# Loading the gate weights in a thread of their own, and letting the first output tile begin before the last head's weights are ready

## The chip, the cores and the metric

The kernel runs on one core of a Trainium2 chip. The metric is the device time of one execution in microseconds (us). Three runs of the kernel before gave 402.6, 404.37 and 405.15; their median is 404.37. The engines are TensorE (PE, with PEld for its weight loads), VectorE (DVE), ScalarE (ACT), GpSimd (POOL) and SyncE (SP), which issues the DMAs here.

## The reference, cut to what matters

One layer that runs differential attention (four heads) and a bidirectional S5 state-space model (SSM) side by side over 512 sample tokens and 128 prompt tokens of 1024 channels. The change touches only the end of the layer:

```python
m = silu(cond) @ w_ada + b_ada                  # shift, scale, gate = thirds of m, one set for
                                                # the sample tokens and one for the prompt tokens
w = softmax(q1 k1) - lam * softmax(q2 k2)       # per head
o = rmsnorm(w @ v, subln) * (1 - lam_init) * silu(g_attn)            # 512 channels, four heads
ys = ys * sigmoid(ys @ w_glu + b_glu) * silu(g_ssm)                  # 512 channels, the SSM gate
out = concat([o, ys]) @ w_out                   # 640 x 1024 times 1024 x 1024
y = x + gate * rmsnorm(out, norm_post)
```

The gate's weights (`w_gate` in the kernel) are the last third of `w_ada`, 1024 x 1024 in fp32, that is eight blocks of 512 KB. `w_out` and `x` are read in blocks of 512 KB too, eight of `w_out` and five of `x`.

## The kernel before, in words

**Threads and the planner.** The program is a list of some fifty generators ("threads"), each with a priority number (line 1572 ff.; lower goes first). When the kernel is built, a planner (`Machine.run`) asks every thread for its next instruction, works out with a table of its own costs when that could start, and takes the earliest; among those that are within a small tie it takes the lowest priority number. What comes out is one fixed order of instructions for each engine. On the chip every engine keeps to its order and only waits for data. A thread waits in the planner for events (`yield from on(...)`), which another thread sets with `did(...)`.

**Memory.** SBUF is cut into named regions; `sb(..., at="T1 T2")` takes room in the first of these regions where the planner finds it free, `drop` gives it back. The eight PSUM banks are handed out by `bank(...)` and given back by `undo`. The profile shows tiles by region (`sb_T`, `sb_S`, `sb_RAW`, ...), and every engine instruction has line 270 there, since a single helper records them all; tiles tell them apart.

**Around the change.** Late in the program these threads run side by side:
- `scores`, `values`, `finish`: for each of four heads, score blocks of 128 rows, a softmax on ACT and DVE, transposes of the weights, products with the values (128x128 matmuls `sb_T,sb_WH`), then the norm of the head's result on DVE and ACT, four transposes back (`sb_S,sb_WH`), the gating, and a split into two parts. Event `("w", h, b)` says that block b of head h has its weights; blocks have another order than their numbers, and `("w", 3, 4)` belongs to the last head.
- `glu`: the gate of the SSM branch; its event is "glu".
- `gates` (line 1427): four rounds. A round loads two `w_gate` blocks (512 KB each) into regions T1 and T2, multiplies each with the conditioning vectors (`ada_mm`, eight matmuls of 32 columns per block, which the trace shows as sixteen rows), adds the bias on DVE, splits the sum on ACT and DVE, spreads it over 128 rows with four selector matmuls of 256 columns (`sb_RX`), and multiplies it on DVE by `norm_post` into `gp`. In each round bias and norm are loaded by two small DMAs of their own, from the same SP queue as everything else.
- `wo_load`, `wo_split`: the eight `w_out` blocks are loaded into RAW, RX or T2 and split into two tiles each. `x_load`: the five blocks of `x` for the residual.
- `output` (line 1497): five output tiles of 128 tokens. The first four have 48 matmuls of 128x512 each: eight input blocks k in `ORDER = (4, 5, 0, 1, 6, 7, 2, 3)`, two halves of the columns, and three products of split numbers (high x high, high x low, low x high). Blocks 4 to 7 of `z` come from the SSM gate, blocks 0 to 3 from the heads, so block 3, the last in the order, waits for the last head. Each tile takes a pair of PSUM banks. `out_after` norms a tile, multiplies by `gp`, adds `x` and stores it.

The last head's result passes: the last value matmul, a copy on DVE, a sum of squares on ACT, twelve small DVE instructions for its norm, three scalings, four transposes, the gating, the split, and then the six matmuls of block 3 in the first output tile.

Of the kernel before, what the change touches and what calls it, by code (L numbers as in the profile page):

```python
# [11 lines left out]
OP = mybir.AluOpType  # L12
# [334 lines left out]
def layer(m, pst, dr, I, O, V, A, P, S, T):  # L347
    sizes = {}

    def sb(*shape, dt=F32, at="S", low=True, step=1):  # L350
        n = -(-math.prod(shape) // 8) * 8
        ap, at = yield lambda: m.take(n, dt, at.split(), low, step)
        sizes[at] = n
        ap = ap[:, 0:math.prod(shape)]
        if dt == I32:
            ap = ap.bitcast(dt)
        if len(shape) > 1:
            nm = "abcd"[:len(shape)]
            ap = ap.rearrange("p (%s) -> p %s" % (" ".join(nm), " ".join(nm)), **dict(zip(nm[1:], shape[1:])))
        return ap  # L360

    def sbs(n, *shape, **k):
        o = []
        for _ in range(n):
            o.append((yield from sb(*shape, **k)))
        return o

    def drop(*aps):
        for ap in aps:
            at = m.box(ap)[0]  # L370
            m.give(at, sizes.pop(at))
# [105 lines left out]
    g = {}  # L477
# [949 lines left out]
    def gates():  # L1427
        yield from on(("w_q", 3, 1), ("v", 1, 2))
        gp = g["gpost"] = yield from sb(2, 1024, at="T1", low=False)
        sel = yield from sb(2, 128)  # L1430
        bt, npo = yield from sbs(2, 256, at="T1", low=False)
        yield S.dma_start(sel, I["sel"])
        yield V.memset(bt, 0.0)
        sr, hi, lo = yield from sbs(3, 256, dt=F32R, at="RX")
        yield A.activation(sr, flat(sel), AF.Copy)
        drop(sel)
        for i in range(4):
            r = slice(256 * i, 256 * i + 256)
            yield S.dma_start(bt[0:2], bass.AP(tensor=I["b_gate"].tensor, offset=I["b_gate"].offset + 256 * i,
                                               ap=[[0, 2], [1, 256]]))  # L1440
            yield S.dma_start(npo, bass.AP(tensor=I["npost"].tensor, offset=I["npost"].offset + 256 * i,
                                           ap=[[0, 128], [1, 256]]))
            ps = yield from bank((4, 5, 6, 7))
            for j in range(2):
                wa = yield from sb(8, 128, at="T1 T2")
                yield S.dma_start(wa, I["w_gate"][2 * i + j])
                yield from ada_mm(ps[:, 128 * j:128 * j + 128], wa, 128)
                drop(wa)
            rg = yield from sb(256)
            yield V.tensor_tensor(rg, ps[:, 0:256], bt, op=OP.add)  # L1450
            undo(ps)
            yield from split(hi, lo, rg)
            drop(rg)
            ps = yield from bank((4, 5, 6, 7))
            for v in range(2):
                o = ps[:, 256 * v:256 * v + 256]
                for n, x in enumerate((hi, lo)):
                    yield T.matmul(o, sr[:, 128 * v:128 * v + 128], x, start=(n == 0), stop=(n == 1))
            yield V.tensor_tensor(gp[:, :, r], ps.rearrange("p (a b) -> p a b", a=2),
                                  npo[:, None].to_broadcast([128, 2, 256]), op=OP.mult)  # L1460
            undo(ps)
        drop(bt, npo, sr, hi, lo)
        did("gates")


    ORDER = (4, 5, 0, 1, 6, 7, 2, 3)
# [28 lines left out]
    later3 = []  # L1495

    def output():
        yield from on("glu", ("w", 3, 4))
        for t in range(5):
            q = slice(128 * t, 128 * t + 128)  # L1500
            if t == 3:
                yield from on("gates")
            pr = yield from bank((0, 2, 4, 6), pair=True)
            ps = [pr[:, 0], pr[:, 1]]
            if t < 4:
                order = [(n, c) for n in range(8) for c in PIECE[t]]
            else:
                order = [(n, c) for c in PIECE[t] for n in range(8)]
                ps.append((yield from bank((0, 1, 2, 3, 4, 5, 6, 7))))
            ps = [p[:, 0:c.stop - c.start] for p, c in zip(ps, PIECE[t])]  # L1510
            for n, c in order:
                k = ORDER[n]
                yield from on(("z", k), ("wo", k))
                yield from three(ps[PIECE[t].index(c)], [x[:, q] for x in g["z", k]], [x[:, c] for x in g["wo", k]], n == 0,
                                 n == 7)
                if n == 7:
                    did(("out", t, c.start))
                    if c == PIECE[t][1 if t < 4 else 0]:
                        later3.append(out_after(t, ps))
# [45 lines left out]
    def trailing3():  # L1565
        for _ in range(5):
# [5 lines left out]
            (4.0, g_make()), (-2.0, g_turn()), (2.0, follow("g_turn", 16)), (5.0, g_apply()), (4.0, follow("g_apply", 16)), (-8.0, scan()), (0.0, fin()),  # L1572
            (1.0, e_make()), (3.0, e_taps()), (2.0, tz_make()), (0.0, y_in()), (1.0, y_out()), (-2.0, follow("y_out", 8)), (11.0, w_load()), (4.0, w_split()), (13.0, proj()),
            (0.0, trailing()), (TURN, turn()), (5.0, lam_()), (1.0, keys()), (-2.0, scores()), (8.0, values()), (5.0, finish()), (14.0, glu()),
            (2.0, trailing2()), (8.0, gates()), (11.0, wo_load()), (20.0, wo_split()), (24.0, x_load()), (13.0, output()), (9.0, trailing3())]

# [91 lines left out]
```

## Time and profile before

| | |
|---|---|
| runs (median) | 402.6, 404.37, 405.15 us (404.37) |
| the profiled execution | 403.84 us, its span 401.7 us |
| granted TensorE clock, mean over the span | 0.987 |
| PE busy | 377.9 us, 94% of the span |
| DVE busy | 338.1 us, 84% |
| ACT busy | 212.4 us, 53% |
| POOL busy | 19.7 us, 5% |
| DMA | 50.80 MB in the span |

A time in the rows counts from the start of the span, which is shorter than the time of the execution: what lies before its first and behind its last instruction is not in it. Rows of the timelines join neighbouring instructions of one kind (x3 is three of them): the first number is the start of the first, the second the length of the whole piece. Consecutive matmuls overlap, so the step from one piece's start to the next one's tells more than its length.

### The profile page before, as it was taken

To read this page: it belongs to the slowest core of one execution; us is meant where nothing else is said; L and a number is where in the kernel's file an instruction comes from. 1 tells how busy PE (TensorE), PEld (TensorE's weight loads), DVE (VectorE), ACT (ScalarE), POOL (GpSimd) and SP (SyncE) were. 2 spreads that over 40 slices of the span, in tenths; PEclk is the share of its full clock that TensorE was granted. 3 is DMA by queue.
4 is the path that set the end of the run, shared out by engine and by line. 5 is a ranking of instruction groups with operands and counts; after the bars stand their busy time and mean duration, and the time that the engine had idled before them with its cause. 6 is when DMAs were issued, how large, how long until landed. Compare 5 with 4: busy or idle time off the path is not lost.

```text
span 401.7 us, 8863 instructions
## 1 busy us (share of the span) xinstructions
PE 377.9 (94%) x3422; PEld 336.0 (84%) x3422; DVE 338.1 (84%) x964; ACT 212.4 (53%) x473; POOL 19.7 (5%) x30
## 2 busy tenths in 40 slices
PE   6899999999999999999999999999999877999991
PEld 6887899987988889999989899898977755788891
DVE  4999899998999998999999997899988986633453
ACT  4766556599823252323584565798874872311021
POOL 1101000000000000000000220032000020000001
PEclk9899999999999999999999999999999998999998
DMA  7999127540354232131186411054023535132111
GB/s 277 404 407 364 48 60 216 180 130 3 104 164 105 80 131 85 60 104 54 56 194 170 119 35 27 11 187 131 25 87 115 157 130 214 52 106 104 52 54 52
DMA packets 30969, 50.80 MB, mean 126 GB/s; under 512 B 11592, under 2 KB 19792, under 8 KB 29904
## 3 DMA queue, kind: packets, MB, share of 16 engines
q1 hardware_dynamic: 30928, 50.24, 38.6%
q8 instruction: 27, 0.44, 0.5%
q14 instruction: 14, 0.11, 0.1%
HBM read 43.45 MB, written 6.78 MB: 125 GB/s over the span
## 4 chain that ended last, share of the span: by engine, by line
PE 58%; DVE 23%; DMA 10%; ACT 4%; issue 3%; SPq 1%; DVEq 0%; ACTq 0%
PE ps__65 L270 58%; DVE sb_S L270 13%; DMA sb_T<-in_w_gate 7%; ACT sb_WH L270 4%; DVE sb_W L270 3%; DVE sb_WH L270 3%; DMA sb_H<-in_x 1%; DMA sb_RAW<-in_w_gs 1%; DMA sb_S<-dk 1%; DVE sb_Z L270 1%; DVE sb_BC L270 1%; SPq L270 1%; DVE sb_T L270 0%; ACT sb_S L270 0%; DVE sb_RX L270 0%
## 5 line engine op out<-in xcount | busy, mean ns | idle before, releaser
L270 PE MATMUL ps__65<-sb_H,sb_W 128*128 128x320 f32 x864 | 141.9, 316 | 0.0
L270 PEld LDWEIGHTS ps__65<-sb_H,sb_W 128*128 128x128 f32 x864 | 127.7, 188 | 2.7 <-issue 1.4
L270 ACT ACTIVATE sb_WH<-ps__65 128x128 f32<-128x128 f32 (+4 forms) x89 | 39.9, 483 | 32.4 <-PE ps__65 L270 30.7
L270 PE MATMUL ps__65<-sb_H,sb_Z 128*128 128x256 f32 (+2 forms) x247 | 49.1, 332 | 0.0
L270 ACT ACTIVATE sb_W<-sb_RAW 128x1024 fp32r<-128x1024 f32 (+1 forms) x26 | 26.2, 1011 | 40.6 <-PE ps__65 L270 30.5
L270 PEld LDWEIGHTS ps__65<-sb_H,sb_Z 128*128 128x128 f32 x247 | 38.7, 190 | 4.8 <-issue 2.0
L270 DVE TENSOR_REDUCE sb_S<-ps__65 128x1 f32<-128x640 f32 (+2 forms) x48 | 29.5, 622 | 5.0 <-PE ps__65 L270 3.2
L270 ACT ACTIVATE sb_WH<-ps__65,sb_S 128x640 f32<-128x640 f32 (+2 forms) x46 | 31.0, 683 | 4.2 <-DVE sb_S L270 4.0
L270 PE MATMUL ps__65<-sb_S 64*128 64x320 f32 (+2 forms) x258 | 30.5, 320 | 1.0 <-POOL sb_S L270 1.0
L270 PE MATMUL ps__65<-sb_W,sb_S 128*32 128x256 f32 (+2 forms) x184 | 27.6, 378 | 3.8 <-DVE sb_S L270 3.8
L270 DVE TENSOR_TENSOR sb_W<-sb_RAW,sb_W 128x1024 fp32r<-128x1024 f32 (+1 forms) x25 | 28.9, 1155 | 0.1
L270 PE MATMUL ps__65<-sb_S,sb_WH 128*128 128x128 f32 x136 | 26.3, 289 | 2.6 <-DVE sb_S L270 1.3
L270 PEld LDWEIGHTS ps__65<-sb_S 64*128 64x128 f32 (+1 forms) x258 | 25.3, 200 | 3.9 <-issue 1.8
L270 PE MATMUL ps__65<-sb_W,sb_H 128*128 128x512 f32 x120 | 28.3, 392 | 0.0
L270 PEld LDWEIGHTS ps__65<-sb_W,sb_H 128*128 128x128 f32 x120 | 22.3, 188 | 4.7 <-issue 0.2
L270 DVE TENSOR_TENSOR sb_S<-sb_S 128x512 f32<-128x512 f32 (+7 forms) x67 | 20.0, 303 | 7.1 <-DMA sb_S<-in_spar 4.5
L270 PEld LDWEIGHTS ps__65<-sb_W,sb_S 128*32 128x32 f32 (+1 forms) x184 | 18.5, 148 | 8.6 <-DVE sb_S L270 3.9
L270 DVE TENSOR_TENSOR sb_WH<-ps__65,sb_T 128x512 f32<-128x512 f32 (+1 forms) x10 | 6.6, 665 | 21.3 <-ACT sb_RAW L270 15.4
L270 PEld LDWEIGHTS ps__65<-sb_S,sb_WH 128*128 128x128 f32 x136 | 17.1, 152 | 8.4 <-ACT sb_WH L270 3.5
L270 ACT ACTIVATE sb_T<-ps__65 128x512 f32<-128x512 f32 (+2 forms) x31 | 14.9, 490 | 17.4 <-PE ps__65 L270 16.9
L270 DVE SCALAR_TENSOR_TENSOR sb_S<-sb_S 128x1 f32<-128x1 f32 (+5 forms) x117 | 20.3, 186 | 2.4 <-ACT sb_S L270 1.1
L270 DVE SCALAR_TENSOR_TENSOR sb_WH<-sb_WH,sb_S 128x640 f32<-128x640 f32 (+3 forms) x29 | 22.0, 771 | 0.4
(146 smaller groups left out, 624.5 us busy)
## 6 DMA issues: line engine op xcount, KB each, us to landing
sb_W<-in_w_ada SPq DMA_DIRECT2D x6, 1024.0 KB, 11.7
sb_T<-in_w_gate SPq DMA_DIRECT2D x8, 512.0 KB, 4.7
sb_RAW<-in_w_out SPq DMA_DIRECT2D x7, 512.0 KB, 3.8
sb_H<-in_x SPq DMA_DIRECT2D x5, 512.0 KB, 5.1
sb_WH<-in_x SPq DMA_DIRECT2D x5, 512.0 KB, 5.7
sb_T<-in_w_ada SPq DMA_DIRECT2D x2, 1024.0 KB, 13.6
sb_RAW<-in_w_k SPq DMA_DIRECT2D x4, 512.0 KB, 3.3
sb_RAW<-in_w_q SPq DMA_DIRECT2D x4, 512.0 KB, 3.4
```

The source lines that it names most:

```text
L270: r = getattr(self.eng[op.eng], op.name)(*op.args, **op.kw)
```

## The change

Three things are changed in two threads, and one thread is added.
- Bias and norm are loaded once: the norm as a whole row of 1024 straight into the tile `gp`, before the loops, and the bias as one tile of four rows of 256 columns, cleared by a memset that goes from DVE to POOL. The multiply with the norm becomes two instructions per round, of 256 columns each, since its result now overwrites the norm.
- The `w_gate` loads move to a thread `gates_load` with the same priority (8.0), which starts when the room for bias and norm is taken and has no other condition but room in T1 or T2.
- `output` waits for "glu" alone; the wait for `("w", 3, 4)` moves from the first to the second tile. The first tile may now take only banks 4 and 5.

```diff
--- before.py
+++ after.py
@@ -1427,27 +1427,26 @@
     def gates():
         yield from on(("w_q", 3, 1), ("v", 1, 2))
         gp = g["gpost"] = yield from sb(2, 1024, at="T1", low=False)
-        sel = yield from sb(2, 128)
-        bt, npo = yield from sbs(2, 256, at="T1", low=False)
+        yield S.dma_start(gp[:, 0], bass.AP(tensor=I["npost"].tensor, offset=I["npost"].offset, ap=[[0, 128], [1, 1024]]))
+        sel, bt = (yield from sb(2, 128)), (yield from sb(4, 256))
         yield S.dma_start(sel, I["sel"])
-        yield V.memset(bt, 0.0)
+        yield P.memset(bt, 0.0)
+        yield S.dma_start(bt[0:2], bass.AP(tensor=I["b_gate"].tensor, offset=I["b_gate"].offset,
+                                           ap=[[0, 2], [256, 4], [1, 256]]))
+        did("gates room")
         sr, hi, lo = yield from sbs(3, 256, dt=F32R, at="RX")
         yield A.activation(sr, flat(sel), AF.Copy)
         drop(sel)
         for i in range(4):
             r = slice(256 * i, 256 * i + 256)
-            yield S.dma_start(bt[0:2], bass.AP(tensor=I["b_gate"].tensor, offset=I["b_gate"].offset + 256 * i,
-                                               ap=[[0, 2], [1, 256]]))
-            yield S.dma_start(npo, bass.AP(tensor=I["npost"].tensor, offset=I["npost"].offset + 256 * i,
-                                           ap=[[0, 128], [1, 256]]))
             ps = yield from bank((4, 5, 6, 7))
             for j in range(2):
-                wa = yield from sb(8, 128, at="T1 T2")
-                yield S.dma_start(wa, I["w_gate"][2 * i + j])
+                yield from on(("wg", 2 * i + j))
+                wa = g["wgate", 2 * i + j]
                 yield from ada_mm(ps[:, 128 * j:128 * j + 128], wa, 128)
                 drop(wa)
             rg = yield from sb(256)
-            yield V.tensor_tensor(rg, ps[:, 0:256], bt, op=OP.add)
+            yield V.tensor_tensor(rg, ps[:, 0:256], bt[:, i], op=OP.add)
             undo(ps)
             yield from split(hi, lo, rg)
             drop(rg)
@@ -1456,11 +1455,18 @@
                 o = ps[:, 256 * v:256 * v + 256]
                 for n, x in enumerate((hi, lo)):
                     yield T.matmul(o, sr[:, 128 * v:128 * v + 128], x, start=(n == 0), stop=(n == 1))
-            yield V.tensor_tensor(gp[:, :, r], ps.rearrange("p (a b) -> p a b", a=2),
-                                  npo[:, None].to_broadcast([128, 2, 256]), op=OP.mult)
+            for v in (1, 0):
+                yield V.tensor_tensor(gp[:, v, r], ps[:, 256 * v:256 * v + 256], gp[:, 0, r], op=OP.mult)
             undo(ps)
-        drop(bt, npo, sr, hi, lo)
+        drop(bt, sr, hi, lo)
         did("gates")
+
+    def gates_load():
+        yield from on("gates room")
+        for n in range(8):
+            wa = g["wgate", n] = yield from sb(8, 128, at="T1 T2")
+            yield S.dma_start(wa, I["w_gate"][n])
+            did(("wg", n))
 
 
     ORDER = (4, 5, 0, 1, 6, 7, 2, 3)
@@ -1495,12 +1501,14 @@
     later3 = []
 
     def output():
-        yield from on("glu", ("w", 3, 4))
+        yield from on("glu")
         for t in range(5):
             q = slice(128 * t, 128 * t + 128)
             if t == 3:
                 yield from on("gates")
-            pr = yield from bank((0, 2, 4, 6), pair=True)
+            if t == 1:
+                yield from on(("w", 3, 4))
+            pr = yield from bank((0, 2, 4, 6) if t else (4,), pair=True)
             ps = [pr[:, 0], pr[:, 1]]
             if t < 4:
                 order = [(n, c) for n in range(8) for c in PIECE[t]]
@@ -1572,7 +1580,7 @@
             (4.0, g_make()), (-2.0, g_turn()), (2.0, follow("g_turn", 16)), (5.0, g_apply()), (4.0, follow("g_apply", 16)), (-8.0, scan()), (0.0, fin()),
             (1.0, e_make()), (3.0, e_taps()), (2.0, tz_make()), (0.0, y_in()), (1.0, y_out()), (-2.0, follow("y_out", 8)), (11.0, w_load()), (4.0, w_split()), (13.0, proj()),
             (0.0, trailing()), (TURN, turn()), (5.0, lam_()), (1.0, keys()), (-2.0, scores()), (8.0, values()), (5.0, finish()), (14.0, glu()),
-            (2.0, trailing2()), (8.0, gates()), (11.0, wo_load()), (20.0, wo_split()), (24.0, x_load()), (13.0, output()), (9.0, trailing3())]
+            (2.0, trailing2()), (8.0, gates()), (8.0, gates_load()), (11.0, wo_load()), (20.0, wo_split()), (24.0, x_load()), (13.0, output()), (9.0, trailing3())]
 
 
 
```

What this does to the order of instructions is seen at three places. The first is SP's queue from the load of the last cached keys (`in_kc`) on, before and now (`sb_T` and `sb_RAW` are where the blocks go):

```order
L270 DMA sb_S_78<-in_kc 128x128
L270 DMA sb_T_0_188<-in_w_gate 128x1024
L270 DMA sb_T_0_91<-in_w_gate 128x1024
L270 DMA sb_T_0_91<-in_b_gate 2x256
L270 DMA sb_T_0_91<-in_npost 128x256
L270 DMA sb_T_0_91<-in_w_gate 128x1024
L270 DMA sb_T_0_188<-in_w_gate 128x1024
```

```order
L270 DMA sb_S_78<-in_kc 128x128
L270 DMA sb_S_78<-in_sel 128x256
L270 DMA sb_RAW_105<-in_w_out 128x1024
L270 DMA sb_S_78<-in_b_gate 2x1024
L270 DMA sb_T_0_91<-in_w_gate 128x1024
L270 DMA sb_T_0_188<-in_w_gate 128x1024
L270 DMA sb_RAW_105<-in_w_out 128x1024
L270 DMA sb_T_0_91<-in_w_gate 128x1024
L270 DMA sb_T_0_188<-in_w_gate 128x1024
L270 DMA sb_T_0_91<-in_w_gate 128x1024
L270 DMA sb_T_0_188<-in_w_gate 128x1024 x3
L270 DMA sb_WH_79<-in_x 128x1024 x3
```

The first two `w_gate` loads now stand behind the seventh `w_out` load and the bias load; the last four stand together, with three loads of `x` right behind, and no bias or norm load is left among them.

The second place is PE from the last value matmul on (the first row of each piece). Moving tiles `sb_H_1_518`, `sb_W_1_707`, `sb_W_1_753` and `sb_H_1_253` with 512 columns are `w_out` blocks of the first output tile, rows of 32 columns are gate matmuls, `sb_RX` rows the selector matmuls, and `sb_S_78,sb_WH_79` transposes. Before, and now:

```order
L270 MATMUL ps__65<-sb_T_0_188,sb_WH_79 128x128
L270 MATMUL ps__65<-sb_H_1_518,sb_S_1_2565 128x512 x6
L270 MATMUL ps__65<-sb_H_1_518,sb_Z_3157 128x512
L270 MATMUL ps__65<-sb_W_1_707,sb_Z_3157 128x512
L270 MATMUL ps__65<-sb_H_1_518,sb_Z_3157 128x512
L270 MATMUL ps__65<-sb_T_0_91,sb_S_78 32x128 x3
L270 MATMUL ps__65<-sb_S_78,sb_WH_79 128x128
L270 MATMUL ps__65<-sb_T_0_91,sb_S_78 32x128 x5
L270 MATMUL ps__65<-sb_H_1_518,sb_Z_3157 128x512
```

```order
L270 MATMUL ps__65<-sb_T_0_188,sb_WH_79 128x128
L270 MATMUL ps__65<-sb_W_1_753,sb_S_1_2821 128x512
L270 MATMUL ps__65<-sb_H_1_253,sb_S_1_2821 128x512
L270 MATMUL ps__65<-sb_W_1_753,sb_S_1_2821 128x512
L270 MATMUL ps__65<-sb_RX_3679 128x256
L270 MATMUL ps__65<-sb_H_1_253,sb_S_1_2821 128x512
L270 MATMUL ps__65<-sb_RX_3679 128x256 x3
L270 MATMUL ps__65<-sb_H_1_253,sb_S_1_2821 128x512 x3
L270 MATMUL ps__65<-sb_T_0_91,sb_S_78 32x128 x8
L270 MATMUL ps__65<-sb_H_1_253,sb_S_1_2821 128x512 x2
L270 MATMUL ps__65<-sb_T_0_188,sb_S_78 32x128 x8
L270 MATMUL ps__65<-sb_S_78,sb_WH_79 128x128 x4
```

Before, 42 of the first tile's 48 matmuls stood behind the last value matmul. Now 9 stand between it and the last head's four transposes, with the gate matmuls of the fifth and sixth `w_gate` block among them, and 6 behind.

The third place is PE at the start of the first output tile, now (before, that tile's first matmuls stood between the last transposes of attention weights, a few rows ahead of the last value matmul). `sb_S_1_2821 128x320` are the matmuls of score blocks:

```order
L270 MATMUL ps__65<-sb_S_1_2821 128x320 x12
L270 MATMUL ps__65<-sb_T_0_188,sb_WH_79 128x128
L270 MATMUL ps__65<-sb_S_78,sb_WH_79 128x128
L270 MATMUL ps__65<-sb_H_1_518,sb_Z_3157 128x512 x6
L270 MATMUL ps__65<-sb_H_1_518,sb_S_1_2565 128x512 x5
L270 MATMUL ps__65<-sb_S_78,sb_WH_79 128x128 x4
L270 MATMUL ps__65<-sb_H_1_518,sb_S_1_2565 128x512
L270 MATMUL ps__65<-sb_S_1_2821 128x320 x12
```

The tile's first twelve matmuls stand ahead of one of the last head's score blocks, and more of them between the softmax work behind it: 33 of 48 come before the last value matmul.

## Rows read from the trace of the kernel before

**Rows 1.** The page's head and its busy times by engine.
```profile
span 401.7 us, 8863 instructions
PE 377.9 (94%) x3422; PEld 336.0 (84%) x3422; DVE 338.1 (84%) x964; ACT 212.4 (53%) x473; POOL 19.7 (5%) x30
```

**Rows 2.** The chain of waits in order of time: start, length, what.
```profile
329.37 7.21 DMA sb_T<-in_w_gate
336.62 9.22 PE ps__65 L270 x59
...
348.14 45.09 PE ps__65 L270 x220
```

**Rows 3.** PE's timeline: start, length, operation, out<-in, shapes, count, [idle before <-releaser].
```profile
329.52 0.94 PE L270 MATMUL ps__65<-sb_H,sb_Z 128*128 128x512 f32 x3
...
331.55 0.38 PE L270 MATMUL ps__65<-sb_T,sb_WH 128*128 128x128 f32 x2
...
343.14 0.64 PE L270 MATMUL ps__65<-sb_T,sb_S 128*32 128x128 f32 x16
...
345.23 0.60 PE L270 MATMUL ps__65<-sb_S,sb_WH 128*128 128x128 f32 x4
...
349.19 1.55 PE L270 MATMUL ps__65<-sb_H,sb_Z 128*128 128x512 f32 x6
...
358.74 1.52 PE L270 MATMUL ps__65<-sb_H,sb_UY 128*128 128x512 f32 x6
360.10 1.52 PE L270 MATMUL ps__65<-sb_H,sb_Z 128*128 128x512 f32 x6
```

**Rows 4.** PE's waits from 285 us on: us in total, times, longest.
```profile
PE ps__65 L270 <- DMA sb_T<-in_w_gate: 5.7, 5, 2.6
PE ps__65 L270 <- DVE sb_S L270: 1.3, 1, 1.3
PE ps__65 L270 <- ACT sb_WH L270: 0.5, 1, 0.5
PE ps__65 L270 <- DVE sb_WH L270: 0.4, 1, 0.4
```

**Rows 5.** Stretches: length, PE busy (count), granted clock, DMA share, GB/s.
```profile
320.00:334.00 14.00, 11.09 (x90) 1.00 0.49 160
336.70:340.00 3.30, 3.30 (x20) 0.50 0.40 158
```

**Rows 6.** The w_gate loads as one tile: from issue to landing.
```profile
DMA to landing us min/median/max: 3.4/4.7/7.2
```

**Rows 7.** SP's timeline, the issues of loads.
```profile
289.35 0.33 SPq L270 DMA_DIRECT2D sb_T<-in_w_gate  x1
...
317.05 0.33 SPq L270 DMA_DIRECT2D sb_RAW<-in_w_out  x1
```

**Rows 8.** POOL's groups: busy us and mean ns | idle before.
```profile
L270 POOL MEMSET sb_S<- 128x400 f32 (+1 forms) x3 | 0.9, 357 | 0.3 <-POOLq L1656 0.3
```

**Rows 9.** DVE's timeline around the last head's end.
```profile
333.07 0.28 DVE L270 COPY sb_WH<-ps__65 128x128 f32<-128x128 f32 x1
...
344.39 0.17 DVE L270 SCALAR_TENSOR_TENSOR sb_S<-sb_S 128x5 f32<-128x5 f32 x1
344.59 0.68 DVE L270 TENSOR_SCALAR sb_WH<-sb_WH,sb_S 128x128 f32<-128x128 f32 x3
...
345.87 0.75 DVE L270 SCALAR_TENSOR_TENSOR sb_S<-ps__65,sb_S,sb_S 128x512 f32<-128x512 f32 x1 [0.26 <-PE ps__65 L270]
...
347.39 0.69 DVE L270 TENSOR_TENSOR sb_UY<-sb_S,sb_UY 128x512 fp32r<-128x512 f32 x1
```

**Rows 10.** ACT's timeline around the last head's end.
```profile
333.39 0.31 ACT L270 ACTIVATE sb_S<-sb_WH 128x128 f32<-128x128 f32 x1 [0.60 <-DVE sb_WH L270]
333.61 0.19 ACT L270 ACTIVATION_READ_ACCUMULATOR sb_S<-sb_WH 128x1 f32 x1
...
346.65 0.63 ACT L270 ACTIVATE sb_UY<-sb_S 128x512 fp32r<-128x512 f32 x1 [1.28 <-DVE sb_S L270]
```

## The prediction, made before the changed kernel was run

> **What bounds the kernel now.** I read the engines' busy times first, then the chain of waits at its end, then PE's waits, and last the timelines of PE, SP, DVE and ACT around the last head. PE is busy 94% of a span of 401.7 us [rows 1]; the profiled execution took 403.84 us, so 2.14 lie around the span. A kernel like this gets faster only where PE idles, runs slowly, or has its last work made ready late.
>
> The chain ends with one unbroken PE stretch of 45.09 us from 348.14 on, and it goes through w_gate loads before that [rows 2]. The stretch is the second output tile (from 349.19 [rows 3]) and the three after it. The change touches neither these four tiles, but for some matmuls of the gates, nor the 8.5 us behind them. So **its worth is how far it moves the start of the second tile**, now 349.19.
>
> What happens ahead of it? From 285 us on PE waits 5.7 us for w_gate loads in five waits, the longest 2.6, and 1.3 + 0.5 + 0.4 = 2.2 us for DVE and ACT [rows 4]. [...]
>
> **The change, part by part.** *Loads of bias and norm.* Four norm loads and four bias loads become one each. In the old order a norm load stood in the queue just ahead of three of the w_gate pairs; the last of these w_gate loads, issued at 329.37, took 7.21 us to land [rows 2], where the quickest took 3.4 and the median was 4.7 [rows 6]. Six issues of about 0.33 us [rows 7] leave SP, which is no bound. The gain of this edit sits in the waits above.
>
> *The loading thread.* It does not bring the first loads forward. They were issued from 289.35 on; now the queue has the seventh w_out load, and then the bias load, ahead of them. The w_out load waits for DVE to free its buffer, which was at 317.05 [rows 7]. In the new order of DVE that release stands one of the last head's row maxima earlier, so I take 313 to 314 us; the first w_gate issues some 0.8 later and lands at 314.4 + 3.4 to 4.7 = 317.8 to 319.1. PE comes to the first group of gate matmuls just ahead of the last-but-one score block, about 318 to 319. So this wait is nothing to 1 us; I take zero, the upper end stays in the range. Loads 5 to 8 leave when PE frees their buffers, about ten matmuls before they are used.
>
> *The memset on POOL.* Three memsets of up to 400 columns took POOL 0.36 us on average [rows 8]; for 1024 that is at most about 1 us. It is off DVE, and SP waits for w_out at that time anyway. If that cover goes, up to 1 us comes onto the loads. The four multiplies by the norm, one of 512 columns each, become eight of 256: nothing but a start each, beside PE.
>
> *The first tile earlier.* Its 48 matmuls of 128x512 used to start at 329.52 and surround the last value matmul at 331.55 [rows 3]: 6 before it, 42 after. In the new order 33 stand before it and 15 after, 9 of them ahead of the last head's transposes and 6 behind them. Now two things can set the second tile's start, PE's work up to the last value, and the last head's chain after it; I go through both.
>
> Last value: 27 matmuls more at 0.227 us (358.74 to 360.10 for six [rows 3]) are +6.1. Two of the six gate groups that stood before it move behind it, 16 matmuls each taking two rows, 2 x 0.64 = 1.3 [rows 3], and eight selector matmuls of 256 columns at half of 0.227, 0.9. The w_gate waits before it, 5.7 - 2.6 = 3.1, go. The 2.2 of other waits I leave. 331.55 + 6.1 - 1.3 - 0.9 - 3.1 = **332.4**.
>
> Chain behind it: the value matmul 0.38 [rows 3]; DVE's copy 0.28 [rows 9]; ACT's square and its sum, 333.39 to 333.80, 0.41 [rows 10]; twelve small DVE instructions, about 0.2 each with the step to the next, 2.4; three scalings 0.68 [rows 9]; four transposes 0.60 [rows 3]; the gating 0.75 [rows 9]; the split on ACT 0.63 [rows 10] and on DVE 0.69 [rows 9]; six output matmuls 1.36 [rows 3]. That is 8.2. Two gate multiplies now stand among the small DVE instructions, 2 x 0.35 (half of the 0.69): +0.7. Seven handovers of 0.03 (346.62 to 346.65 [rows 9, 10]): +0.2. Together **9.1**. PE has less than this to do meanwhile: 15 x 0.227 + 8 x 0.11 + 2 x 1.28 + 0.6 = 7.5. So the chain, not PE, sets the second tile: 332.4 + 9.1 = 341.5. In the old order the same chain was hidden, since the first tile's other 42 matmuls, a wait and a slow clock lay beside it. The last four selector matmuls now fall inside the second tile: +0.4, so 341.9.
>
> Sum: 349.2 - 341.9 = 7.3 us earlier; 403.84 - 7.3 = **396.5 us**. The profiled execution is 0.53 below the median of the runs shown, 404.37. I forecast 396.6, 1.9% below that median; a measurement here tells 1% (4.0 us, at 400.3 and 408.4) from no change.
>
> Bounds: if the first tile's matmuls also fill the 2.2 us of waits on DVE and ACT, 394.4. [...]
>
> [...]
>
> **Rivals.**
> *Loads 5 to 8 land late.* Four w_gate loads and the first x loads, 512 KB each, follow each other as PE frees the buffers. With a landing of 7.2 us in place of 3.4, as the last group had, PE stands 2.6 us in the gate matmuls ahead of the last transposes, and the half clock costs 1.7 again: 396.6 + 2.6 + 1.7 = 400.9. For it: the same crowd of x loads follows. Against: no norm load is ahead of them now, and 1.6 us of the wait would lie beside the chain, 9.1 against 7.5.
> *The attention comes no earlier.* The first tile holds banks 4 and 5 from its start, so values, finishing and gates share two banks, and DVE is 84% busy [rows 1]. Then taking away 3.1 us of PE waits only turns them into waits on DVE, and the last value falls at 335.5: 399.7.
> *Nothing is gained.* The waits come back in full elsewhere: 403.8.
> *Slower.* The first loads are stuck behind the seventh w_out load in SP's order. If that load issues at 317 again or later, loads 1 and 2 land after PE needs them, 3 and 4 follow only when PE has used 1 and 2, and 5 to 8 only after these: three rounds in a row, each with a landing in view, while scores and values of the last head stand behind the gates on PE. Three times 3.4 to 4.7 us and one half clock, 1.7: 396.6 + 11.9 to 15.8 = 408.5 to 412.4. It decides from the point where the w_out load leaves SP after about 316. Against it: the release stands earlier in DVE's order, and other work lies between the rounds.
>
> **How the numbers follow.** The forecast (395 to 399) has 0.52, late loads 0.24, attention no earlier 0.10, nothing gained 0.06, slower 0.08. Faster by over 1% is the forecast, a third of the late loads and over half of the attention case: 0.66. Within 1%: the rest of these and nothing gained, 0.26. Slower 0.08. The range runs from the lower bound, 394.0, over the late loads and their 1 us at the first group, to 402.0; nothing gained and slower stay outside, with some of the forecast's own error.
>
> **What would show it.** Right: the second tile starts near 342; PE waits for w_gate under 2 us in sum; the clock stays at 1.00 from 300 to 393; the first w_gate issues after 312 and PE still finds it landed; before the last transposes and before the last six matmuls of the first tile PE waits on DVE for about 1.5 us in all; the four tiles behind still take 44 us. Wrong: a wait of 2 us or more on w_gate with 0.50 behind it, a last value after 334, or the seventh w_out load after 316.

## The result: 399.0 us against 403.9, and the profile after

Four runs of the changed kernel gave 398.54 to 399.24 us, median 399.0; the kernel before ran beside it and has a median of 403.88. The ratio is 0.9878, 95% interval 0.9843 to 0.9913: 4.9 us faster, where the forecast's sum had 7.3. The forecast was 396.6, in a range from 394.0 to 402.0. Six more runs in a later series (e11) gave 398.92 against 404.16, ratio 0.9885 (0.9851 to 0.9919).

The page's head and busy times of the changed kernel, which answer to [rows 1]:

```profile
span 397.4 us, 8857 instructions
PE 376.1 (95%) x3422; PEld 335.7 (84%) x3422; DVE 337.9 (85%) x969; ACT 212.4 (53%) x472; POOL 17.5 (4%) x30
```

The work is the same. PE's waits from 285 us on (us in total, times, longest), beside [rows 4]:

```profile
PE ps__65 L270 <- DVE sb_S L270: 2.1, 2, 1.2
PE ps__65 L270 <- DVE sb_WH L270: 1.0, 2, 0.8
PE ps__65 L270 <- DMA sb_T<-in_w_gate: 0.6, 1, 0.6
PE ps__65 L270 <- ACT sb_WH L270: 0.4, 1, 0.4
```

The waits for `w_gate` fell from 5.7 us to 0.6. In their place PE now waits 3.1 us for DVE, where it waited 1.7. The granted clock tells what that costs (stretch, length, PE busy, clock, DMA share, GB/s), beside [rows 5]:

```profile
300.00:324.00 24.00, 21.64 (x180) 1.00 0.40 133
324.90:328.70 3.80, 3.76 (x20) 0.56 0.00 0
328.70:345.00 16.30, 15.32 (x156) 1.00 0.62 227
```

The half clock of the kernel before, behind its longest `w_gate` wait (0.50 for 3.3 us [rows 5]), is gone, and another one of 3.8 us is there, at a place where no load is under way. PE's timeline shows what led to it, and the places that answer to [rows 3]:

```profile
322.67 0.33 PE L270 MATMUL ps__65<-sb_S,sb_WH 128*128 128x128 f32 x1 [0.77 <-DVE sb_WH L270]
324.15 0.46 PE L270 MATMUL ps__65<-sb_S,sb_WH 128*128 128x128 f32 x2 [1.16 <-DVE sb_S L270]
...
325.16 2.07 PE L270 MATMUL ps__65<-sb_T,sb_WH 128*128 128x128 f32 x8
...
330.95 1.06 PE L270 MATMUL ps__65<-sb_T,sb_WH 128*128 128x128 f32 x8
...
334.57 0.47 PE L270 MATMUL ps__65<-sb_T,sb_WH 128*128 128x128 f32 x2
...
340.56 0.75 PE L270 MATMUL ps__65<-sb_RX 128*128 128x256 f32 x3 [0.94 <-DVE sb_S L270]
...
344.10 1.11 PE L270 MATMUL ps__65<-sb_H,sb_Z 128*128 128x512 f32 x4
```

Two waits on DVE, 0.77 and 1.16 us, stand close together, with one transpose between them; then the same eight value matmuls take 2.07 us, at 0.50 of the clock, in place of 1.06 us at 1.00. 334.57 is the last value matmul, 344.10 the start of the second tile, which was 349.19. DVE's timeline at the second of these waits names what PE waited for:

```profile
322.53 1.22 DVE L270 TENSOR_TENSOR sb_H<-sb_RAW,sb_H 128x1024 fp32r<-128x1024 f32 x1
323.66 0.15 DVE L270 RECIPROCAL sb_S<-sb_S 128x1 f32<-128x1 f32 x1
```

The split of the last `w_out` block goes just ahead of a softmax step. It begins only near the end of the first wait, so it can be the reason of the second alone.

One thing more has to be known before the two profiled executions are set side by side. The third of the four loads of cached keys stands at the same place of SP's order in both, ahead of everything that the change moves. In the kernel before and in the changed one it was issued at

```profile
255.77 0.33 SPq L270 DMA_DIRECT2D sb_S<-in_kc  x1
```

```profile
257.68 0.33 SPq L270 DMA_DIRECT2D sb_S<-in_kc  x1
```

So this run came 1.91 us late to the place where the change begins. Over the fourteen profiled executions of this study that load lies between 254.85 and 257.68, and the change has no part in it: e11, a second execution of the changed kernel, has 254.90. The cause is open. The clock from 10 to 20 us was lower here (0.66 against 0.83 on average), but e3 and e7, with 0.83, came as late (257.62 and 257.67). Where a place is compared with the kernel before, the text says what it is less this difference.

### The profile page after: what moved, and what is told of

Read it like the earlier page. It is cut to its first block, busy times and chain, and to the rows that moved or that the text cites. A ratio compares the mean times of both kernels' runs of the same rounds, so it can differ in the third digit from the quotient of the medians.

```text
span 397.4 us, 8857 instructions
## 1 busy us (share of the span) xinstructions
PE 376.1 (95%) x3422; PEld 335.7 (84%) x3422; DVE 337.9 (85%) x969; ACT 212.4 (53%) x472; POOL 17.5 (4%) x30
## 4 chain that ended last, share of the span: by engine, by line
PE 73%; DVE 14%; ACT 5%; DMA 4%; issue 3%; SPq 1%; DVEq 0%; POOL 0%; POOLq 0%; ACTq 0%
PE ps__65 L270 73%; DVE sb_S L270 9%; ACT sb_WH L270 4%; DVE sb_WH L270 3%; DMA sb_H<-in_x 1%; DMA sb_T<-in_w_gate 1%; DVE sb_W L270 1%; DMA sb_S<-dk 1%; ACT sb_S L270 1%; SPq L270 1%; DVE sb_BC L270 0%; DVE sb_Z L270 0%; DVE sb_RX L270 0%; DVE sb_H L270 0%; DVEq L1667 0%
## 5 line engine op out<-in xcount | busy, mean ns | idle before, releaser
L270 ACT ACTIVATE sb_WH<-ps__65 128x512 f32<-128x512 f32 (+5 forms) x95 | 43.5, 490 | 49.4 <-PE ps__65 L270 48.5
L270 ACT ACTIVATE sb_W<-sb_RAW 128x1024 fp32r<-128x1024 f32 (+1 forms) x25 | 25.2, 1010 | 40.3 <-PE ps__65 L270 32.9
L270 PE MATMUL ps__65<-sb_W,sb_S 128*32 128x256 f32 (+2 forms) x184 | 29.9, 403 | 5.1 <-DVE sb_S L270 5.0
L270 DVE SCALAR_TENSOR_TENSOR sb_S<-sb_S 128x1 f32<-128x1 f32 (+5 forms) x117 | 19.4, 178 | 2.4 <-ACT sb_S L270 1.1
```

The lines of the kernel that those rows point to most:

```text
L270: r = getattr(self.eng[op.eng], op.name)(*op.args, **op.kw)
```

## The experiments

Three kinds of question were asked: which part of the change carries the gain (e1 to e4), what in the loads it is (e5 to e7, e9), and what the early tile and the thread do beside it (e8, e10 to e12). In the table "once" means bias and norm loaded once. The series e1 to e4, e5 to e8 and e9 to e12 each ran beside the kernel before on a chip of their own, so the ratio compares better between them than the median.

| | what it is | median us | ratio to before, 95% interval |
|---|---|---|---|
| changed | once + thread + early tile | 399.0 | 0.9878 (0.9843 to 0.9913) |
| e11 | the same again | 398.92 | 0.9885 (0.9851 to 0.9919) |
| e1 | once + thread | 398.41 | 0.9865 (0.9837 to 0.9893) |
| e2 | early tile alone | 405.63 | 1.0038 (1.0012 to 1.0064) |
| e3 | once | 398.63 | 0.9874 (0.9842 to 0.9906) |
| e4 | once + early tile | 396.48 | 0.9828 (0.9798 to 0.9858) |
| e12 | the same again, beside e11 | 396.16 | 0.9803 (0.9777 to 0.9828) |
| e5 | norm load behind the `w_gate` loads | 401.98 | 0.9927 (0.9894 to 0.9961) |
| e6 | norm once, alone | 398.93 | 0.9878 (0.9836 to 0.992) |
| e7 | bias once, alone | 405.58 | 1.0054 (1.002 to 1.0087) |
| e9 | thread alone | 398.5 | 0.9863 (0.9837 to 0.9889) |
| e8 | changed, last split held back | 401.67 | 0.9944 (0.9917 to 0.9971) |
| e10 | norm once + early tile | 401.85 | 0.9933 (0.9908 to 0.9958) |

**e1: the loads without the early tile.**

```diff
-        yield from on("glu")
+        yield from on("glu", ("w", 3, 4))
...
-            if t == 1:
-                yield from on(("w", 3, 4))
-            pr = yield from bank((0, 2, 4, 6) if t else (4,), pair=True)
+            pr = yield from bank((0, 2, 4, 6), pair=True)
```

> The changed kernel with its output thread as before: the first output tile waits for the last head's weights again and may take any bank pair. Theory A (both parts are needed: the early tile fills PE while the last heads' softmax is worked out, the loads take away the waits for w_gate): the w_gate waits after 285 us fall from 5.7 to about 1 us, but without the early tile PE waits 3 to 5 us for VectorE and ScalarE around the last head's scores, and the granted clock falls there; 400.5 to 403. Rival B (the loads alone are the gain): 398.5 to 399.5, as the changed kernel. Rival C (the early tile alone is the gain): 403 to 405.

Measured: 398.41. PE waited for no `w_gate` load after 285 us. It did wait 4.4 us in sum for ACT and DVE, as theory A had it, but 0.8 at most at a time, and the granted clock was 1.00 from 285 to 392 us.

**e2: the early tile without the loads.** The kernel before with the other side of e1's diff.

> The kernel before with only its output thread changed: the first tile may begin with the SSM gate done and takes banks 4 and 5; bias, norm and gate weights are loaded as before. Theory A: the w_gate loads are still issued round by round, so PE still waits 4 to 6 us for them after 285 us, and one wait with a half clock behind it stays; 400.5 to 403.5. Rival B (the loads alone): 403 to 405. Rival C (the early tile alone): 398.5 to 399.5.

Measured: 405.63, slower than the kernel before and above every line expected. PE's waits:

```profile
PE ps__65 L270 <- DMA sb_T<-in_w_gate: 4.8, 4, 1.8
PE ps__65 L270 <- DVE sb_S L270: 0.9, 1, 0.9
```

The loads are waited for as before, and the last head's chain, which the first tile's matmuls used to hide, is now waited for as well (0.9 us, with a half clock behind it from about 347.2 to past 350). Theory A and rival C fall with these two: the early tile is not needed for the gain, and alone it costs.

**e3: bias and norm once, without thread and early tile.** e1's diff, and the loads back in the rounds:

```diff
-                yield from on(("wg", 2 * i + j))
-                wa = g["wgate", 2 * i + j]
+                wa = yield from sb(8, 128, at="T1 T2")
+                yield S.dma_start(wa, I["w_gate"][2 * i + j])
```

> Only bias and norm loaded once (one 128x1024 load and one bias load, memset on POOL, two multiplies); the gate weights are loaded inside the rounds again and the output thread is as before. In the new order of SP the first w_gate load stands behind both last w_out loads, and x loads stand between the w_gate rounds. Theory A: the waits for w_gate stay at 4 to 6 us or grow, 402 to 406. Rival B in its narrow form (fewer small loads are the gain): 399 to 400.

Measured: 398.63. This small edit alone gives the gain of the changed kernel; theory A expected 402 or more. Not every wait went: in the profiled execution, the slowest of its six (400.13), PE still waited 1.6 us for `w_gate`, 0.7 at most at a time.

**e4: bias and norm once, and the early tile.** The changed kernel with e3's diff alone.

> The changed kernel without the loading thread: bias and norm once, the early first tile, but each round of the gates loads its own two w_gate blocks. Theory A: the loads come late, PE waits 2 to 5 us for w_gate between the last head's scores and the second tile, 400 to 403. If the thread adds nothing to the other two parts: 398.5 to 399.5.

Measured: 396.48, below the runs so far and below what either line expected. The thread did not only add nothing: beside the early tile it costs.

Why do two kinds of loads, one of 256 columns and one of two rows, carry 5 us? Three stretches of the kernel before answer it. DVE's multiplies with the norm:

```profile
299.28 0.69 DVE L270 TENSOR_TENSOR sb_T<-ps__65,sb_T 128x512 f32<-128x512 f32 x1
...
311.90 0.69 DVE L270 TENSOR_TENSOR sb_T<-ps__65,sb_T 128x512 f32<-128x512 f32 x1
...
328.25 0.67 DVE L270 TENSOR_TENSOR sb_T<-ps__65,sb_T 128x512 f32<-128x512 f32 x1
```

and SP's issues:

```profile
300.00 0.34 SPq L270 DMA_DIRECT2D sb_T<-in_npost  x1
300.44 1.70 SPq L270 DMA_DIRECT2D sb_T<-in_w_gate  x2
...
312.62 0.33 SPq L270 DMA_DIRECT2D sb_T<-in_npost  x1
313.07 0.36 SPq L270 DMA_DIRECT2D sb_T<-in_w_gate  x1
...
328.95 0.33 SPq L270 DMA_DIRECT2D sb_T<-in_npost  x1
329.37 0.38 SPq L270 DMA_DIRECT2D sb_T<-in_w_gate  x1
```

Each multiply ends (299.97, 312.59, 328.92) 0.03 us before a norm load is issued, and the `w_gate` loads follow 0.4 us later. The norm has one buffer. Its load for the next round may not start until the round before has been multiplied, which is that round's last step, and SP, which keeps to its order, holds the `w_gate` loads behind it. The rounds run one after the other, each with a load in view. I call this theory D. Its rival E was the order of the whole queue: with both loaded once, the rounds begin near 312 us and behind the `w_out` loads, not near 289.

**e5: the norm load behind the `w_gate` loads of its round.**

```diff
-            yield S.dma_start(npo, bass.AP(tensor=I["npost"].tensor, offset=I["npost"].offset + 256 * i,
-                                           ap=[[0, 128], [1, 256]]))
             ps = yield from bank((4, 5, 6, 7))
...
+            yield S.dma_start(npo, bass.AP(tensor=I["npost"].tensor, offset=I["npost"].offset + 256 * i,
+                                           ap=[[0, 128], [1, 256]]))
             rg = yield from sb(256)
```

> The kernel before with one thing moved: in each round the norm load (128x256, its own single buffer) is issued behind the two w_gate loads of the round and not ahead of them. No DMA fewer, same buffers, output thread as before. Theory D (the norm load has to wait until VectorE has multiplied with the norm of the round before, and holds the w_gate loads behind it in SP's queue): the w_gate loads leave SP some 1 to 4 us earlier, PE's waits for w_gate fall from 5.7 to under 3 us and the slow clock behind the longest goes; 399 to 401. Theory E (with bias and norm loaded once the rounds of the gates simply begin 20 us later, behind the w_out loads, and that order is the gain): here the rounds begin as early as before, 403 to 405.

Measured: 401.98, half a step, and above the 399 to 401 of theory D; its runs spread from 398.4 to 405.4. In the profiled one (399.61) PE waited 0.3 us for `w_gate`, but 2.5 for DVE, and the clock was at half twice, from about 319.1 to 322.5 and from 325.9 to 329.4. The waits for `w_gate` went as D says; others took their place, and why they did here and not in e6 was not found.

**e6: the norm once, alone.** The norm part of the change on the kernel before; bias per round, no thread, no early tile.

> The kernel before with the norm alone loaded once (128x1024 into the gate tile), bias per round as before. Theory D: the wait behind VectorE's multiply is gone, 398.5 to 400.5. Theory E: the rounds still begin near 290 us, ahead of the last three w_out loads, so 403 to 405.

Measured: 398.93. SP's issues in the third round:

```profile
307.06 0.26 SPq L270 DMA_DIRECT2D sb_T<-in_b_gate  x1
307.41 0.81 SPq L270 DMA_DIRECT2D sb_T<-in_w_gate  x2
```

They leave 5.7 us earlier than the 313.07 of before, 4.7 less the early start of this execution (its keys were loaded at 254.85), though the bias is loaded per round still, and none is waited for. The rounds begin at 288 us, as in the kernel before (289), so E falls.

**e7: the bias once, alone.** The bias part of the change on the kernel before; the memset goes to POOL with it.

> The kernel before with the bias alone loaded once (2x1024 into a tile of 1024 columns cleared by POOL), norm per round and ahead of the w_gate loads as before. The order of SP now has all w_out loads ahead of the first round. Theory D: the norm load still holds the w_gate loads of three rounds, PE waits 4 to 6 us for them, 402 to 405. Theory E: 398 to 399.5, like bias and norm together (398.6).

Measured: 405.58, 0.5% slower than the kernel before. The queue has E's order, with all `w_out` loads ahead, and the norm's chain too (SP's issues of the second round, then PE's waits):

```profile
331.07 0.33 SPq L270 DMA_DIRECT2D sb_T<-in_npost  x1
331.50 0.85 SPq L270 DMA_DIRECT2D sb_T<-in_w_gate  x2
```

```profile
PE ps__65 L270 <- DMA sb_T<-in_w_gate: 8.2, 4, 2.8
```

Of these 8.2 us the first wait is not D's, since no round has been multiplied before it; the other three, 1.80, 1.66 and 1.94, stand behind such a load. The first tells something else:

```profile
320.89 0.65 PE L270 MATMUL ps__65<-sb_T,sb_S 128*32 128x128 f32 x16 [2.78 <-DMA sb_T<-in_w_gate]
```

It is longer than the 2.63 of the kernel before, which had a half clock behind it, and here no half clock follows, neither behind this wait nor behind the other three: the clock is 1.00 from 285 to 388 us. A half clock behind such a wait is thus no certainty.

**e9: the loading thread alone,** bias and norm per round in their single buffers.

```diff
         yield V.memset(bt, 0.0)
+        did("gates room")
...
-                wa = yield from sb(8, 128, at="T1 T2")
-                yield S.dma_start(wa, I["w_gate"][2 * i + j])
+                yield from on(("wg", 2 * i + j))
+                wa = g["wgate", 2 * i + j]
...
+    def gates_load():
...
```

> The kernel before with the loading thread alone: the w_gate loads come from a thread of their own, bias and norm are loaded per round into their single buffers as before, the output thread is as before. In the new order of SP a pair of w_gate loads stands ahead of the norm load that waits for VectorE, not behind it. Theory D (the norm load's wait holds the w_gate loads behind it): this is another way to take the chain apart, PE's waits for w_gate fall from 5.7 to under 2 us, 398.5 to 401. Rival (only fewer loads help, not their order): 403 to 405.

Measured: 398.5, with no wait for `w_gate` after 285 us; `gates_load` is that of the change. The norm loads still wait for DVE, but a pair of `w_gate` loads now stands ahead of each:

```profile
304.42 0.81 SPq L270 DMA_DIRECT2D sb_T<-in_w_gate  x2
306.53 0.26 SPq L270 DMA_DIRECT2D sb_T<-in_b_gate  x1
311.40 0.33 SPq L270 DMA_DIRECT2D sb_T<-in_npost  x1
```

Here too the clock was at half for 3.4 us (about 340.9 to 344.4), behind waits on DVE of 0.87 and 0.94 us in the last head's chain, and the time is 398.5 all the same.

Edits that cut the same link (e3 or e6, e9, and both in e1) give 398.4 to 398.9; the one that loads less but leaves it (e7) gives nothing. D stands, with e5 as the case where cutting the link gave only half, and thread and "once" are two cures of one ill: together they gain no more than either.

**e8: the changed kernel with the last split held back.**

```diff
             yield from on(("wor", k))
+            if k == 3:
+                yield from on(("w", 3, 4))
             hi, lo = yield from sbs(2, 1024, dt=F32R, at="H1 W1 W2 W3 H2")
```

> The changed kernel, with the split of the last w_out block (ACT copy and a 1.22 us subtraction on VectorE) held back until the last head's weights are done. Theory F (in the changed kernel this split stands in VectorE's order just ahead of the reciprocal and the scalings that the last head's transposes wait for; PE's waits of 0.77 and 1.16 us come from it, and so does the stretch of some 4 us at half clock behind them): both waits shrink and the clock stays at 1.00 from 300 to 390, 396.3 to 397.5. Rival G (the loading thread costs by its late w_gate loads and the wait on POOL's memset, not by VectorE): no change, 398.5 to 399.5.

Measured: 401.67, slower than the changed kernel, which neither theory expected. Clock and waits of PE:

```profile
320.00:330.00 10.00, 8.61 (x84) 1.00 0.46 158
...
340.00:350.00 10.00, 8.78 (x38) 0.68 0.25 79
```

```profile
338.69 0.72 PE L270 MATMUL ps__65<-sb_S,sb_WH 128*128 128x128 f32 x4 [1.14 <-DVE sb_WH L270]
...
342.00 0.55 PE L270 MATMUL ps__65<-sb_RX 128*128 128x256 f32 x1 [1.21 <-DVE sb_S L270]
```

The clock stays at 1.00 from 320 to 330, as theory F has it. That does not show the split as the cause, since the changed kernel's second execution (e11) has 1.00 there too, with the split in its place. And the gate matmuls that used to lie beside the last head's chain have moved forward, PE waits 1.14 and 1.21 us in that chain, and the half clock comes there, for longer (about 339.5 to 346.3). A hole that was filled opened further on. Theory F is neither shown nor refuted.

**e10: the norm once, and the early tile.** e6 with the early tile.

> The norm loaded once (as in the run with the norm alone, 398.9) and the early first tile on banks 4 and 5; bias per round, no loading thread. If the early tile is worth 2 us wherever the norm no longer holds the loads (as it was beside bias and norm once without the thread: 398.6 to 396.5): 396 to 397.5. If that gain was bound to the late rounds that the bias tile makes: 398.5 to 400.

Measured: 401.85, that is 2.9 above e6 and above both lines expected. PE at the last head's transposes, and the clock there:

```profile
341.20 0.63 PE L270 MATMUL ps__65<-sb_S,sb_WH 128*128 128x128 f32 x4 [2.26 <-ACT sb_WH L270]
342.76 0.45 PE L270 MATMUL ps__65<-sb_S,sb_WH 128*128 128x128 f32 x1 [0.94 <-DVE sb_S L270]
```

```profile
340.00:350.00 10.00, 7.75 (x23) 0.66 0.31 125
```

The early tile's matmuls are used up before the last head is done, the gates are done too, and nothing is left beside its chain: 2.26 + 0.94 us of waits and nearly 7 us at half clock.

**e11 and e12: the changed kernel and e4 again, side by side.**

> The changed kernel once more, beside the others on one chip. If 399.0 of its first four runs is typical: 398.5 to 399.5, and the profile shows PE's two waits on VectorE and the half clock near 325 us again. If these runs had a late start by chance (half clock until 17.7 us, 1.9 us behind the kernel before ahead of any changed instruction): 397 to 398.

> The changed kernel without the loading thread once more, on the same chip as the changed kernel. If the thread costs 2.5 us: 396 to 397 where the changed kernel has 398.5 to 399.5. If the difference was between chips or runs: both within 1 us.

Measured: 398.92 and 396.16. 399.0 was typical, and without the thread the kernel is 2.8 us faster in the same series: the best version of this study, 0.9803 of the kernel before. Its clock in the whole stretch (three windows):

```profile
300.00:320.00 20.00, 19.72 (x165) 1.00 0.39 133
320.00:340.00 20.00, 17.73 (x175) 1.00 0.61 211
340.00:345.00 5.00, 5.00 (x25) 1.00 0.00 0
```

There is no half clock, though PE waits here as well: its single waits from 300 us on are 0.64 at most. The second profile of the changed kernel shows more waits than the first. Beside the same two waits of 0.77 and 1.16 us it shows two on `w_gate`:

```profile
314.65 0.65 PE L270 MATMUL ps__65<-sb_T,sb_S 128*32 128x128 f32 x16 [1.28 <-DMA sb_T<-in_w_gate]
...
336.19 0.64 PE L270 MATMUL ps__65<-sb_T,sb_S 128*32 128x128 f32 x16 [1.11 <-DMA sb_T<-in_w_gate]
```

The clock stayed full behind the two DVE waits this time, and fell later, from about 338.3 to 341.7, behind the second `w_gate` wait and one of 0.93 us on DVE. So the same pair of waits was followed by a half clock in one execution and not in the other, and the half clock near 325 us that was expected again did not come.

## Why the prediction was right, and where its sum was off

**What bounds the kernel** was read rightly: the four tiles behind still take one unbroken stretch, and the worth is the start of the second tile. From there to the end of the span it is 53.3 us (397.4 - 344.10) after 52.5 before; 0.4 of the 0.8 more was forecast, for the selector matmuls.

**The start of the second tile** was forecast at 341.5, or 341.9 with the 0.4 of selector matmuls that fall into the tile. It came at 344.10. Less the 1.91 of the late start it is 342.2, and the change moved it by 7.0 us in that pair of executions; in e11's it came at 343.17, with its load of keys at 254.90, so 5.2. To the end of the span the change then kept 6.2 us in the first pair and 4.4 in e11's, where 7.3 were forecast; the medians, 4.9 and 5.2, lie between. Whether the varying start has a part in the medians is not known, since only profiled executions show it.

**The step that failed** is the price of PE's waits. 2.2 us were kept for waits on DVE and ACT and none for a half clock behind them. The prediction counted one only in two of its rivals, at 1.7 us, which is what [rows 5] show for the kernel before: 3.3 us at 0.50 behind the wait of 2.6 us. In the first profile of the changed kernel the DVE waits of 0.77 and 1.16 us were followed by 3.8 us at 0.56 of the clock, 1.7 us lost; in e11 later waits did it, of 1.11 and 0.93 us, with 3.4 us at half. So two shorter ones close together were enough in these executions, and a longer one was not in another (2.78 us in e7). Every half clock seen between 300 and 350 us in these profiles stands behind waits of PE (the longest of them from 0.88 us in e5 to 2.63 in the kernel before), but 1.13 us in e6 and 1.16 in e11 were followed by none. What decides whether one follows was not shown.

**The last value matmul** was forecast at 332.4 and came at 334.57, less the late start 332.66; in e11 at 331.26, with its early start taken into account 332.1. That it fits is partly luck. These are the stretches from the load of keys to the last value, before and changed:

```profile
255.77:331.55 75.78, 69.65 (x601) 1.00 0.35 112
```

```profile
257.68:334.57 76.89, 73.30 (x588) 0.98 0.30 99
```

PE's idle time fell by 2.5 us (from 6.13 to 3.59), where the sum took off 3.1. Its busy time rose by 3.65, of which 1.7 are the half clock, so by 2.0, where the sum added 6.1 - 1.3 - 0.9 = 3.9. The work ahead was thus counted some 1.9 us too high, and that hid the half clock and a `w_gate` wait of 0.6. The 13 rows fewer are those of the sum (27 more, 32 and 8 fewer), so a price in it is wrong and not a count; which one, no run here tells.

**The chain behind it** was forecast at 9.1 us and took 9.53 (344.10 - 334.57), but not as forecast. PE's stretch, and a row that stands between the fifth and the sixth of the last six matmuls of the first tile:

```profile
334.57:344.10 9.53, 8.59 (x95) 1.00 0.97 359
```

```profile
342.75 1.08 PE L270 MATMUL ps__65<-sb_T,sb_S 128*32 128x128 f32 x32
```

"The chain, not PE, sets the second tile" was wrong for most of it: PE was busy for 8.59 us, where 7.5 were counted, and waited once, 0.94 us on DVE. To the first of the six matmuls it took 6.80 us (341.37), where the chain had 7.7; from there on 2.73, where the chain had 1.36, mostly because the last two gate groups stand in between. The two errors nearly cancel. In e11, with waits of 1.11 and 0.93 us and the half clock, the same piece took 11.91 us.

**The loads.** The seventh `w_out` load left at 310.48 (308.57 less the late start; forecast 313 to 314), the first `w_gate` load at 312.26, and PE waited 0.58 us for it, inside the "nothing to 1 us" of the text, and in e11 1.28, above it. Part of it is the memset, whose cover was gone. SP's and POOL's rows:

```profile
310.48 0.33 SPq L270 DMA_DIRECT2D sb_RAW<-in_w_out  x1
311.89 0.31 SPq L270 DMA_DIRECT2D sb_S<-in_b_gate  x1
312.26 0.81 SPq L270 DMA_DIRECT2D sb_T<-in_w_gate  x2
```

```profile
310.91 0.95 POOL L270 MEMSET sb_S<- 128x1024 f32 x1 [2.31 <-ACT sb_S L270]
```

The bias load waited for the memset, 1.1 us after the `w_out` issue had ended, and the `w_gate` loads behind it. The text gave it up to 1 us. The rival "slower", with the loads stuck behind the `w_out` load in three rounds, was not seen. "Loads 5 to 8 land late" was, in e11: 1.11 us and a half clock behind. "The attention comes no earlier", whose 399.7 lies nearer to the measured time than the forecast does, was not: it put the last value at 335.5. Of the prediction's own signs of being wrong, "a last value after 334" came up as the profile reads (334.57), but not less the late start; the clock did not stay at 1.00 from 300 on, which was a sign of being right.

**What the prediction did not see** is where its own gain sits. It said that a norm load stood just ahead of three of the `w_gate` pairs and counted its issue; that this load waits for the multiply of the round before, and holds the queue, it did not say, though SP's and DVE's timelines show it to 0.03 us. Its sum does not part the loads from the early tile. The runs give the whole measured gain to the loads: cutting the tie to one small load is enough, by the norm alone (e6) or by the thread alone (e9). The early tile, on which most of the text went, takes 2.2 us off beside "once" (e3 to e4), adds 0.5 beside the thread (e1 to the changed kernel, inside the intervals), and costs 1.9 and 2.9 in e2 and e10. The text had written that the first tile's 42 matmuls hid the last head's chain, and had not asked what the early tile costs when the gates don't take over that cover: in e10 they don't.

**What stays open:** why the thread costs 2.8 us beside the early tile. In the profiles the waits on DVE (3.1 us in both executions with it against 1.4 in e4 and e12), on `w_gate` (0.6 and 2.4 against 0.5) and the half clock (3.8 and 3.4 us against none) are all larger with it, and in e8, which held back one split, the half clock came at another place. The wait on the memset is in both versions (1.08 us from the end of the `w_out` issue to the bias load, in e12 too). Which of the moved instructions decides was not found.

## What to carry to other kernels

Before costing a small load by its size, look at what it waits for: here a single buffer, refilled in a loop, made the queue wait for the end of the round before, and the `w_gate` loads behind it waited too; a load's issue 0.03 us behind the end of DVE's multiply was the sign. Work that is pulled forward to fill PE leaves a hole where it was: look at which chain it used to hide, and what will hide that chain then (in e10 nothing did, and PE waited 2.26 and 0.94 us). A forecast of PE's waits needs a second line for the clock behind them: here it was 1.7 us lost in the first profile of the changed kernel, and nothing in e7.

## What the runs showed of the hardware

- Half clock behind waits that are short one by one: 0.77 and 1.16 us with one transpose between were followed by 3.8 us at 0.56 in the first profile of the changed kernel and by none in e11, the same kernel. A single wait of 2.63 us was followed by 3.4 us at half in the kernel before, and one of 2.78 us in e7 by none. In e4 and e12, where no wait from 300 to 350 is above 0.64 us, the clock stayed at 1.00.
- The start of the program varies: the clock from 10 to 20 us was 0.66 or 0.67, 0.83 or 1.00 on average in these executions, and the place 256 us on came between 254.85 and 257.68; the one does not give the other (257.62 with 0.83 in e3, 256.28 with 0.67 in e9).
- A memset of 1024 columns by POOL took 0.95 us, where three of up to 400 had taken 0.36 on average [rows 8].
